# Three edits in a hybrid encoder kernel: the softmax division as a ScalarE copy, zero-padded low parts of the RWKV gate matrices, and the attention value projection over 512 columns in four banks

## The chip, the cores and the metric

The kernel runs on one NeuronCore of a Trainium2 chip. The metric is the device time of one execution in microseconds (us), as a median over runs. TensorE (PE in the profile; its weight loads are listed as PEld) multiplies matrices into PSUM, which has eight banks of 128 partitions by 512 float32 numbers. VectorE (DVE) and ScalarE (ACT) work element by element between PSUM and SBUF, GpSimd (POOL) sets constants and issues some of the transfers, and SyncE (SP) issues most of the others. Each engine works through its own list of instructions in order, and waits for others by semaphores.

## The reference, cut to what matters

Two layers over 1024 rows of width 1024. Layer 0 has a combined projection that feeds eight RWKV heads and eight heads of chunked band attention, and an output projection; layer 1 has a convolution module. Each layer ends with a squared-ReLU MLP of width 4096. The edits touch the attention's softmax and values and the decay and gate of RWKV.

```python
proj = h @ w_in
p_rwkv, q, k, v = jnp.split(proj, [RWKV_COLS, RWKV_COLS + ATT_WIDTH, RWKV_COLS + 2 * ATT_WIDTH], axis=-1)
...
w = -jax.nn.softplus(-(w0 + jnp.tanh(xw) @ w2)) - 0.5      # xw, xa: 64 columns each
decay = jnp.exp(-jnp.exp(w.astype(jnp.float32)))
a = jax.nn.sigmoid(a0 + xa @ a2)
...
s = jnp.where(valid[:, None, :], s, -1e30)
probs = jax.nn.softmax(s, axis=-1).astype(v.dtype)
o = jnp.einsum('bhcqk,bckhd->bcqhd', probs, vb)
...
x = x + sq_relu_mlp(rmsnorm(x, g_ffn), up, down)
```

## The kernel before

**Matmuls.** Nearly all matrix products are "dense" ones on split operands: each operand is a high part in a rounded 32-bit format (`xh`, `wh`) and a low part that holds the rest (`xl`, `wl`), and each product is the sum of three matmuls (L270 to L272): high by high, low by high, high by low. A weight part of 128 x 512 numbers arrives by a transfer that SP issues (`wr`), ScalarE rounds it to `wh` (L214), VectorE takes the difference `wl` (L215). Four `wh` and four `wl` buffers stand ready in the first 900 us.

**Halves.** The 1024 rows are worked in two halves of 512. For each half `w_in_gemm` projects the normalized rows: 22 tiles of 128 columns with the weights stationary (`gemm`), and then the attention's values, with the rows stationary and the weights moving, so that the values come out with rows on the partitions (L355 to L379). For the second half, `reload_x` fetches the rows back from DRAM (`xo`, four buffers) and splits them into eight pairs `xh[k]`, `xl[k]` (L163, L164), which take over the eight buffers of the first half's pairs.

**The value projection.** It takes 256 columns at a time. For each, four weight parts (two k steps each) are split, and then four row tiles run over all eight k steps, 24 matmuls of 256 columns each (L369 to L371). Two row tiles share a bank `d`. ScalarE copies each result out with the row's scale (L375) into `t1`, which has two buffers, and POOL writes it to `vd` in DRAM (L378).

**RWKV.** `rwkv` works 16 units in each of which two heads and 256 rows go through three stages (`prep`, `stage2`, `stage3`); the three stages of successive units are emitted interleaved. In `prep` the decay and the gate come from two small products each: `lora[0]` and `lora[1]` hold the rounded matrices w2 and a2, both copied into all 128 partitions, and meet the input's high part in one half of the partitions and its low part in the other (L488). `lora[2]` holds the low parts of both, w2's in partitions 0 to 63 and a2's in 64 to 127, and each product reads its own 64 (L491). `xdt` (the block inverses) and `wx` (the decays) exist twice, for units of even and odd number.

**Attention.** For every pair of heads and every 128 queries: scores of both heads (L808, L810) into a bank `a`, bias and row maximum on VectorE (L812), exponential with row sum on ScalarE (L819), reciprocal of the sum on VectorE (L820), transposes on TensorE (L830) copied out by ScalarE (L831), and products with the values, one head in each half of the columns (L837). The division comes last: a matmul of the reciprocals, broadcast along the columns, with the identity puts them beside the result (L840), ScalarE copies them to SBUF (L843) and VectorE multiplies (L844). Tag `a` has two banks.

**What sets the order.** A list scheduler places every instruction of every engine at build time by four levels: support (weights, evacuations), then the RWKV mixer, then attention, then dense matmuls, which fill what the others leave. `rwkv(0)` and `attention(0)` are emitted ahead of `w_in_gemm(1)`, and `rwkv(1)` and `attention(1)` ahead of the first half's output projection and MLP. Buffers of one tag pass from user to user in the order of the program.

Of the kernel before, what the change touches and what calls it, by code (L numbers as in the profile page):

```python
# [8 lines left out]
F32 = mybir.dt.float32  # L9
# [5 lines left out]
P = 128  # L15
D = 1024
SEQ = 1024
T = 512
# [43 lines left out]
def encoder_trunk(ctx: ExitStack, tc: tile.TileContext, x, vecs, consts, ext, w2a2, g2, w_in, w_out,  # L62
# [17 lines left out]
    def psum(tag):  # L80
        return ps[tag].tile([P, T], F32, tag=tag, name=tag)
# [67 lines left out]
    def boost():  # L149
        return At("support")  # L150

    def tmp(tag="t1"):
        return dpool.tile([P, T], F32, tag=tag, name=tag)
# [181 lines left out]
    def w_in_gemm(h, rhs, st, first=()):  # L335
        def evac(m, q, cols):
            rstd = st.rstd()
            s = tmp("t1")
            if Q0 <= m < K0:
                nc.vector.scalar_tensor_tensor(out=s[:], in0=q[:], scalar=0.125, in1=rstd[:],  # L340
                                               op0=ALU.mult, op1=ALU.mult)
            else:
                nc.vector.tensor_tensor(out=s[:], in0=q[:], in1=rstd[:], op=ALU.mult)
            ts = slice(h * T, (h + 1) * T)
            if Q0 <= m < V0:
                hi = tmp("t2")
                nc.scalar.copy(hi[:].bitcast(F32R), s[:])
                nc.vector.tensor_tensor(out=s[:].bitcast(F32R), in0=s[:], in1=hi[:], op=ALU.subtract)
                nc.gpsimd.dma_start(ph[m][:, ts], hi[:])
                nc.gpsimd.dma_start(pl[m][:, ts], s[:])  # L350
            else:
                nc.gpsimd.dma_start(pd[m][:, ts], s[:])

        gemm(w_in, 0, IN_ORDER, rhs, evac, st, first)
        for n0 in range(V0 * P, V0 * P + RW, 2 * P):  # L355
            parts = []
            with boost():
                for k0 in range(0, KT, 2):
                    parts.append(weight_part(w_in[k0 * P : (k0 + 2) * P, n0 : n0 + 2 * P], 2 * P))
            for t in range(4):  # L360
                if t % 2 == 0:
                    q = psum("d")
                cs = slice(t % 2 * 2 * P, (t % 2 + 1) * 2 * P)
                ts = slice(t * P, (t + 1) * P)
                with At("dense"):
                    for k in range(KT):
                        xh, xl = rhs[k]
                        hi, lo = (a[:].rearrange("p a b -> p (a b)")[:, k % 2 * 2 * P : (k % 2 + 1) * 2 * P] for a in parts[k // 2])
                        nc.tensor.matmul(q[:, cs], xh[:, ts], hi, start=(k == 0), stop=False)  # L369
                        nc.tensor.matmul(q[:, cs], xl[:, ts], hi, start=False, stop=False)  # L370
                        nc.tensor.matmul(q[:, cs], xh[:, ts], lo, start=False, stop=(k == KT - 1))  # L371
                with boost():
                    if t % 2 == 0:
                        s = tmp("t1")
                    nc.scalar.activation(s[:, cs], q[:, cs], AF.Copy, scale=st.part[1][:, t : t + 1])  # L375
                    if t % 2:
                        r0 = h * T + (t - 1) * P
                        nc.gpsimd.dma_start(vd[r0 : r0 + 2 * P, n0 - V0 * P : n0 - V0 * P + 2 * P].rearrange("(a p) c -> p a c", p=P),  # L378
                                            s[:].rearrange("p (a c) -> p a c", a=2))  # L379


    def rwkv(h, rp, nbuf):
        keep = {}
        for i in range(2):
            for n, w in (("xdt", C), ("wx", C + 1)):
                t = rp.tile([P, whole(NCH * w)], F32, tag=f"{n}{i}", name=f"{n}{i}")
                t = keep[n, i] = t[:, 0 : NCH * w].rearrange("p (c t) -> p c t", t=w)
                nc.gpsimd.memset(t, 0.0)
            t = keep["zs", i] = rp.tile([P, 2, C], F32, tag=f"zs{i}", name=f"zs{i}")
            nc.gpsimd.memset(t[:], 0.0)  # L390
# [19 lines left out]
    def rwkv_block(tb, rp, nbuf, keep):  # L410
# [60 lines left out]
        def prep(hp, u):  # L471
# [3 lines left out]
            wx = keep["wx", hp % 2]  # L475
# [13 lines left out]
            for i, q in enumerate((wps, aps)):  # L489
                s = slice(C * i, C * i + C)  # L490
                nc.tensor.matmul(q, lora[2][s, cs], lora_in[i][s, :], start=False, stop=True)  # L491
# [85 lines left out]
        def invert(u):  # L577
# [27 lines left out]
            xd16 = keep["xdt", hp % 2]  # L605
# [143 lines left out]
    def attention(h, ap):  # L749
# [3 lines left out]
        for hp in range(4):  # L753
# [27 lines left out]
            for qi in range(4):  # L781
# [18 lines left out]
                rr = []  # L800
                for hd in range(2):
# [19 lines left out]
                    rr.append(st[:, 4:5])  # L821
# [17 lines left out]
                for hd in range(2):  # L839
                    nc.tensor.matmul(ob[hd * C : hd * C + C, P : 2 * P], rr[hd].to_broadcast([P, C]), ident,  # L840
                                     start=True, stop=True)
                yo = ap.tile([P, P], F32, tag="yo", name="yo", bufs=1)
                nc.scalar.copy(yo[:], ob[:, P : 2 * P])  # L843
                nc.vector.tensor_tensor(out=yo[:], in0=ob[:, 0:P], in1=yo[:], op=ALU.mult)  # L844
# [200 lines left out]
    with banks(d=2, w=2, v=1, c=1, a=2), tc.tile_pool(name="lop", bufs=1) as lop, tc.tile_pool(name="wp1", bufs=4) as wb[0]:  # L1045
        lora = [lop.tile([P, RW], F32R, tag=f"lora{i}", name=f"lora{i}") for i in range(3)]
# [4 lines left out]
        with tc.tile_pool(name="xrp", bufs=4, reuse_waits="tile") as xrp:  # L1051
            with boost():
                xa, ra, sa, first = load_x(0, xrp)
                for i, s in enumerate((slice(0, C), slice(C, P))):
# [4 lines left out]
                    nc.vector.tensor_tensor(out=lora[2][s, :], in0=raw[s, :], in1=lora[i][s, :].bitcast(F32), op=ALU.subtract)  # L1059
# [130 lines left out]
```

## Time and profile before

| what | us |
|---|---|
| median of 3 runs (lowest, highest) | 2507.76 (2507.46, 2511.98) |
| the profiled execution | 2509.98 |
| its span in the profile | 2508.0 |
| PE, DVE, ACT, POOL busy | 2472.3, 1711.5, 1169.2, 118.4 |

In the rows of the profile a group is given as line, engine, operation, output and inputs by tile name, shapes and count; then busy time in us, mean duration of one in ns, and the idle time of the engine just before them with the instruction that ended most of it. For matmuls `128*64` is the stationary operand's rows and columns. A timeline row begins with its start and its duration in us. A float32 matmul that isn't on rounded operands shows as two passes. RWKV, attention and both projections lie in the first 900 us; what follows is MLPs and convolution.

### The profile page before, as it was taken

How to read it: one execution, taken by the hardware profiler on the slowest of the kernel's cores; microseconds unless marked ns; L12 is line 12 of the kernel's file. 1: busy time of each engine (PE TensorE's matmuls, PEld its weight loads, DVE VectorE, ACT ScalarE, POOL GpSimd, SP SyncE). 2: the span in 40 equal slices, each digit the busy share in tenths (PEclk: the TensorE clock that was granted, in tenths of full speed). 3: DMA queues.
4: the chain of work that ended last, by engine and by line, in shares of the span. 5: the costliest groups of instructions: out<-in, count | busy, mean ns of one | idle time of the engine just before them, and what ended most of it. 6: DMA issues, size and time to landing. Idle time of an engine off the chain costs nothing.

```text
span 2508.0 us, 38693 instructions
## 1 busy us (share of the span) xinstructions
PE 2472.3 (99%) x13532; PEld 1983.0 (79%) x13532; DVE 1711.5 (68%) x3559; ACT 1169.2 (47%) x2282; POOL 118.4 (5%) x285
## 2 busy tenths in 40 slices
PE   8999999999999999999999999999999999999998
PEld 6777677787777788888888888888888888888887
DVE  5687775677777644458999956599999475534434
ACT  5456565566775633343442334434432365423324
POOL 1111011100000000001100000000000000000000
PEclk9999999999999999999999999999999999999999
DMA  8543434543233233355333333533333334333332
GB/s 271 161 139 105 128 102 121 184 148 102 82 94 89 72 100 97 97 151 152 98 96 98 96 100 93 161 93 101 93 101 93 101 100 152 93 94 99 97 97 67
DMA packets 478514, 283.46 MB, mean 113 GB/s; under 512 B 44512, under 2 KB 457568, under 8 KB 478320
## 3 DMA queue, kind: packets, MB, share of 16 engines
q1 hardware_dynamic: 468128, 250.25, 34.1%
q0 software_dynamic: 9152, 29.36, 3.3%
q8 instruction: 107, 1.75, 0.3%
q10 hardware_dynamic: 1040, 1.38, 0.2%
q14 instruction: 87, 0.71, 0.1%
HBM read 247.31 MB, written 36.72 MB: 113 GB/s over the span
## 4 chain that ended last, share of the span: by engine, by line
PE 92%; DMA 3%; DVE 2%; ACT 2%; issue 1%; SPq 1%; ACTq 0%; DVEq 0%
PE d L272 26%; PE d L270 25%; PE d L271 25%; PE a L837 1%; PE w L556 1%; PE a L830 1%; PE v L633 1%; PE a L808 1%; DMA pt<-pd 1%; PE c L677 1%; PE c L689 1%; PE c L682 1%; PE a L810 1%; PE d L370 1%; PE d L369 1%
## 5 line engine op out<-in xcount | busy, mean ns | idle before, releaser
L214 ACT CAST wh<-wr 128x512 fp32r<-128x512 f32 x744 | 460.5, 621 | 971.5 <-PE d L271 898.8
L270 PE MATMUL d<-xh,wh 128*128 128x512 f32 x1872 | 743.6, 397 | 3.5 <-ACT xh L163 2.9
L272 PE MATMUL d<-xh,wl 128*128 128x512 f32 x1872 | 741.4, 396 | 1.2 <-DVE wl L215 1.2
L271 PE MATMUL d<-xl,wh 128*128 128x512 f32 x1872 | 739.7, 395 | 0.2 <-DVE xl L164 0.2
L215 DVE TENSOR_TENSOR wl<-wr,wh 128x512 fp32r<-128x512 f32 x744 | 501.6, 685 | 224.8 <-ACT wh L214 169.6
L270 PEld LDWEIGHTS d<-xh,wh 128*128 128x128 f32 x1872 | 353.5, 189 | 76.8 <-ACT xh L163 3.3
L272 PEld LDWEIGHTS d<-xh,wl 128*128 128x128 f32 x1872 | 353.1, 189 | 76.7 <-DVE wl L215 2.5
L271 PEld LDWEIGHTS d<-xl,wh 128*128 128x128 f32 x1872 | 353.5, 189 | 73.0 <-issue 1.2
L270 PE MATMUL d<-mh,wh 128*128 128x512 f32 (+1 forms) x1040 | 404.0, 388 | 0.0
L272 PE MATMUL d<-mh,wl 128*128 128x512 f32 (+1 forms) x1040 | 402.6, 387 | 0.0
L271 PE MATMUL d<-ml,wh 128*128 128x512 f32 (+1 forms) x1040 | 402.3, 387 | 0.0
L964 DVE SCALAR_TENSOR_TENSOR cv<-u,dwt,cv 128x512 f32<-128x512 f32 x480 | 331.9, 743 | 0.7
L272 PEld LDWEIGHTS d<-mh,wl 128*128 128x128 f32 x1040 | 195.3, 188 | 38.8
L270 PEld LDWEIGHTS d<-mh,wh 128*128 128x128 f32 x1040 | 195.3, 188 | 38.7
L271 PEld LDWEIGHTS d<-ml,wh 128*128 128x128 f32 x1040 | 195.4, 188 | 38.6
L863 DVE TENSOR_TENSOR x<-d,x 128x512 f32<-128x512 f32 (+1 forms) x146 | 97.6, 679 | 155.5 <-PE d L272 155.2
L905 DVE SCALAR_TENSOR_TENSOR t<-d,rstd 128x512 f32<-128x512 f32 x128 | 86.4, 687 | 119.6 <-PE d L272 116.8
L911 DVE TENSOR_TENSOR ml<-t,mh 128x512 fp32r<-128x512 f32 x128 | 87.7, 687 | 20.0 <-ACT mh L909 17.3
L907 ACT ACTIVATE t<-t 128x512 f32<-128x512 f32 x128 | 80.1, 626 | 17.9 <-DVE t L905 17.6
L909 ACT ACTIVATE mh<-t 128x512 fp32r<-128x512 f32 x128 | 78.9, 616 | 0.0
L181 DVE TENSOR_TENSOR acc<-acc,t 128x512 f32<-128x512 f32 (+1 forms) x86 | 57.9, 673 | 9.4 <-ACT t L180 9.1
L687 ACT ACTIVATE sd<-vs,dc 64x64 f32<-64x64 f32 x128 | 44.2, 346 | 33.5 <-DVE vs L692 25.8
(265 smaller groups left out, 2439.8 us busy)
## 6 DMA issues: line engine op xcount, KB each, us to landing
wr<-in_up_dram SPq DMA_DIRECT2D x256, 256.0 KB
wr<-in_dn_dram SPq DMA_DIRECT2D x256, 256.0 KB
wr<-in_w_in_dram SPq DMA_DIRECT2D x104, 256.0 KB
wr<-in_pw_dram SPq DMA_DIRECT2D x96, 256.0 KB
wr<-in_w_out_dram SPq DMA_DIRECT2D x32, 256.0 KB
pd<-t POOLq DMA_DIRECT2D x28, 256.0 KB, 2.7
x<-xd SPq DMA_DIRECT2D x24, 256.0 KB
pt<-pd SPq DMA_DIRECT2D x42, 128.5 KB
```

Of the source, the lines that this page charges most:

```text
L181: nc.vector.tensor_tensor(out=self.acc[:, cols], in0=self.acc[:, cols], in1=sq[:, cols], op=ALU.add)
L214: nc.scalar.copy(hi[:], raw[:])
L215: nc.vector.tensor_tensor(out=lo[:], in0=raw[:], in1=hi[:].bitcast(F32), op=ALU.subtract)
L270: nc.tensor.matmul(q[:, cols], hi, xh[:, cols], start=(k == 0), stop=False)
L271: nc.tensor.matmul(q[:, cols], hi, xl[:, cols], start=False, stop=False)
L272: nc.tensor.matmul(q[:, cols], lo, xh[:, cols], start=False, stop=(k == KT - 1))
L863: nc.vector.tensor_tensor(out=xs[m][:, cols], in0=q[:, cols], in1=xs[m][:, cols], op=ALU.add)
L905: nc.vector.scalar_tensor_tensor(out=t[:], in0=q[:], scalar=0.0, in1=rstd[:], op0=ALU.max, op1=ALU.mult)
L907: nc.scalar.activation(sq[:], t[:], AF.Square)
L909: nc.scalar.activation(hi[:], t[:], AF.Square)
L911: nc.vector.tensor_tensor(out=lo[:], in0=sq[:], in1=hi[:].bitcast(F32), op=ALU.subtract)
L964: nc.vector.scalar_tensor_tensor(out=c[:], in0=u[:, tap : tap + T], scalar=dw(tap), in1=c[:], op0=ALU.mult, op1=ALU.add)
```

## The change

Softmax: ScalarE multiplies the exponentials by the reciprocal in place, in SBUF, ahead of the transposes. The 64 matmuls with the identity and ScalarE's copies of their results go, and VectorE's last multiplication becomes a copy out of PSUM.

Gates: the low parts get a tile of their own each, `lora[2]` and `lora[3]`, with zeros in the 64 partitions that hold the input's low part, and the second matmul reads all 128 partitions. To make room, `xdt` and `wx` exist once.

Values: k is the outer loop. Each weight part is 128 rows by all 512 columns, and four accumulators of 512 columns, one per row tile, stay open over all of k, in the two banks `d` and the two banks `a`. Four results of 128 x 512 are copied out at the end.

```diff
         gemm(w_in, 0, IN_ORDER, rhs, evac, st, first)
-        for n0 in range(V0 * P, V0 * P + RW, 2 * P):
-            parts = []
-            with boost():
-                for k0 in range(0, KT, 2):
-                    parts.append(weight_part(w_in[k0 * P : (k0 + 2) * P, n0 : n0 + 2 * P], 2 * P))
-            for t in range(4):
-                if t % 2 == 0:
-                    q = psum("d")
-                cs = slice(t % 2 * 2 * P, (t % 2 + 1) * 2 * P)
-                ts = slice(t * P, (t + 1) * P)
-                with At("dense"):
-                    for k in range(KT):
...
-                    if t % 2 == 0:
-                        s = tmp("t1")
-                    nc.scalar.activation(s[:, cs], q[:, cs], AF.Copy, scale=st.part[1][:, t : t + 1])
...
+        qs = [psum(tag) for tag in SPARE]
+        for k in range(KT):
+            with boost():
+                hi, lo = (a[:].rearrange("p a b -> p (a b)")
+                          for a in weight_part(w_in[k * P : (k + 1) * P, V0 * P : V0 * P + RW], RW))
+            xh, xl = rhs[k]
+            with At("dense"):
+                for t, q in enumerate(qs):
+                    ts = slice(t * P, (t + 1) * P)
+                    nc.tensor.matmul(q[:], xh[:, ts], hi, start=(k == 0), stop=False)
+                    nc.tensor.matmul(q[:], xl[:, ts], hi, start=False, stop=False)
+                    nc.tensor.matmul(q[:], xh[:, ts], lo, start=False, stop=(k == KT - 1))
+        with boost():
+            for t, q in enumerate(qs):
+                s = tmp("t1")
+                nc.scalar.activation(s[:], q[:], AF.Copy, scale=st.part[1][:, t : t + 1])
+                nc.gpsimd.dma_start(vd[h * T + t * P : h * T + (t + 1) * P, :], s[:])
...
-            for i, q in enumerate((wps, aps)):
-                s = slice(C * i, C * i + C)
-                nc.tensor.matmul(q, lora[2][s, cs], lora_in[i][s, :], start=False, stop=True)
+                nc.tensor.matmul(q, lora[2 + i][:, cs], lora_in[i][:], start=False, stop=True)
...
-                    rr.append(st[:, 4:5])
+                    nc.scalar.activation(pt[:, 0:w], pt[:, 0:w], AF.Copy, scale=st[:, 4:5])
...
-                for hd in range(2):
-                    nc.tensor.matmul(ob[hd * C : hd * C + C, P : 2 * P], rr[hd].to_broadcast([P, C]), ident,
-                                     start=True, stop=True)
-                nc.scalar.copy(yo[:], ob[:, P : 2 * P])
-                nc.vector.tensor_tensor(out=yo[:], in0=ob[:, 0:P], in1=yo[:], op=ALU.mult)
+                nc.vector.tensor_copy(yo[:], ob[:, 0:P])
...
-        lora = [lop.tile([P, RW], F32R, tag=f"lora{i}", name=f"lora{i}") for i in range(3)]
+        lora = [lop.tile([P, RW], F32R, tag=f"lora{i}", name=f"lora{i}") for i in range(4)]
+        for i in range(2):
+            nc.gpsimd.memset(lora[2 + i][C - C * i : P - C * i, :].bitcast(F32), 0.0)
...
-                    nc.vector.tensor_tensor(out=lora[2][s, :], in0=raw[s, :], in1=lora[i][s, :].bitcast(F32), op=ALU.subtract)
+                    nc.vector.tensor_tensor(out=lora[2 + i][s, :], in0=raw[s, :], in1=lora[i][s, :].bitcast(F32), op=ALU.subtract)
```

The scheduler's order moves with it. Three places follow. Line numbers of the change are its own: there the value matmuls are L364 to L366, their copies L370, the gate matmuls L480 and L481, scores L797 and L799, exponential L808, the division's copy L810, transposes L819, value products L826.

ACT at the end of the first half's value projection, before: L163 makes the second half's `xh`, L375 copies the last value result, L214 rounds weights, the rest belongs to RWKV and attention.

```order
L680 COPY zs_1658<-c 64x64
L657 COPY vs<-v 128x2x192
L163 ACTIVATE xh<-xo,vec 128x512 x4
L214 CAST wh<-wr 128x512
L375 ACTIVATE t_1480<-d,rc 128x256
L214 CAST wh<-wr 128x512 x2
L163 ACTIVATE xh<-xo,vec 128x512 x2
L214 CAST wh<-wr 128x512
L163 ACTIVATE xh<-xo,vec 128x512 x2
L214 CAST wh<-wr 128x512
```

The same place in the change: the last two of the eight L163 and the four result copies L370, from banks `d` and `a`.

```order
L163 ACTIVATE xh<-xo,vec 128x512
L603 COPY vs<-v 128x2x64
L370 ACTIVATE t_1399<-d,rc 128x512
L370 ACTIVATE t_1402<-d,rc 128x512
L677 ACTIVATE sd<-vs,dc 64x64 x2
L670 COPY zs_1555<-c 64x64
L214 CAST wh<-wr 128x512
L163 ACTIVATE xh<-xo,vec 128x512
L674 COPY vs<-c 64x64
L421 ACTIVATE e<-pt,vec 128x256
L370 ACTIVATE t_1405<-a,rc 128x512
L370 ACTIVATE t_1408<-a,rc 128x512
```

Before, eight splits stand together at the end; now six of them stand further up, among the projection's own weights, and the third and fourth result copies stand behind RWKV's small copies.

PE where the second half's value projection ends, before (the next rows are the first half's output projection):

```order
L369 MATMUL d<-wh,xh 128x256
L370 MATMUL d<-wh,xl 128x256
L371 MATMUL d<-wl,xh 128x256
L270 MATMUL d<-xh,wh 128x512
L271 MATMUL d<-xl,wh 128x512
L272 MATMUL d<-xh,wl 128x512
```

The same place in the change, with L446 of RWKV and the first scores of the second half's attention:

```order
L366 MATMUL a<-wl,xh 128x512
L270 MATMUL d<-xh,wh 128x512
L271 MATMUL d<-xl,wh 128x512
L272 MATMUL d<-xh,wl 128x512
L270 MATMUL d<-xh,wh 128x512
L271 MATMUL d<-xl,wh 128x512
L272 MATMUL d<-xh,wl 128x512
L446 MATMUL w<-cst,e 128x128 x2
L270 MATMUL d<-xh,wh 128x512
L271 MATMUL d<-xl,wh 128x512
L272 MATMUL d<-xh,wl 128x512
L797 MATMUL a<-kk,qq 128x320
```

Before, scores of the second half stand ahead of and inside its value projection; now the first of them follows nine dense matmuls behind it. The first half's last value product stands 60 matmuls of 128x512 ahead of the second half's value projection.

ACT in the second half's attention, before: two exponentials (L819), and the copies of the transposed tiles (L831).

```order
L819 ACTIVATE pt,st<-pt,st 128x640
L684 COPY vs<-c 64x64
L819 ACTIVATE pt,st<-pt,st 128x640
L214 CAST wh<-wr 128x512
L687 ACTIVATE sd<-vs,dc 64x64 x2
L680 COPY zs_6272<-c 64x64
L831 COPY pT<-a 128x512
L831 COPY pT<-a 128x128
```

Such a place in the change, with the division's copies (L810):

```order
L808 ACTIVATE pt,st<-pt,st 128x640
L214 CAST wh<-wr 128x512
L670 COPY zs_6057<-c 64x64
L677 ACTIVATE sd<-vs,dc 64x64 x2
L214 CAST wh<-wr 128x512
L674 COPY vs<-c 64x64
L810 ACTIVATE pt<-pt,st 128x640
L639 COPY bkt<-v 128x512
L808 ACTIVATE pt,st<-pt,st 128x640
L810 ACTIVATE pt<-pt,st 128x640
```

The copy stands after other work behind the first exponential and directly behind the second. On PE, between a head's last score matmul and its first transpose, there stand 22 matmuls of 128x512 in the mean before and 27 now.

More of the change, by code (lines that the diff above doesn't have):

```diff
@@ L354, in w_in_gemm @@
         gemm(w_in, 0, IN_ORDER, rhs, evac, st, first)
-        for n0 in range(V0 * P, V0 * P + RW, 2 * P):
-            parts = []
+        qs = [psum(tag) for tag in SPARE]
+        for k in range(KT):
             with boost():
-                for k0 in range(0, KT, 2):
-                    parts.append(weight_part(w_in[k0 * P : (k0 + 2) * P, n0 : n0 + 2 * P], 2 * P))
-            for t in range(4):
-                if t % 2 == 0:
-                    q = psum("d")
-                cs = slice(t % 2 * 2 * P, (t % 2 + 1) * 2 * P)
-                ts = slice(t * P, (t + 1) * P)
-                with At("dense"):
-                    for k in range(KT):
[L367 to L371, printed above, removed]
-                with boost():
-                    if t % 2 == 0:
-                        s = tmp("t1")
[L375 to L379, printed above, removed]
@@ L382, in rwkv @@
+        with boost():
[3 more added lines that the diff above has]
+                nc.gpsimd.dma_start(vd[h * T + t * P : h * T + (t + 1) * P, :], s[:])
     def rwkv(h, rp, nbuf):
         keep = {}
+        for n, w in (("xdt", C), ("wx", C + 1)):
+            t = rp.tile([P, whole(NCH * w)], F32, tag=n, name=n)
+            t = keep[n] = t[:, 0 : NCH * w].rearrange("p (c t) -> p c t", t=w)
+            nc.gpsimd.memset(t, 0.0)
@@ L384, in rwkv @@
         for i in range(2):
[L385 to L388, printed above, removed]
             t = keep["zs", i] = rp.tile([P, 2, C], F32, tag=f"zs{i}", name=f"zs{i}")
@@ L474, in prep @@
                 yield
-            wx = keep["wx", hp % 2]
+            wx = keep["wx"]
             cs = slice(P * hp, P * hp + P)
@@ L604, in invert @@
                                   xi[C * hd : C * hd + C, :, :].rearrange("p a b -> p (a b)"))
-            xd16 = keep["xdt", hp % 2]
+            xd16 = keep["xdt"]
             for hd in range(2):
@@ L799, in attention @@
                 pr = []
-                rr = []
                 for hd in range(2):
```

## The prediction, made before the result was known

> **What bounds the kernel now.** I read the page first (busy shares and the chain that ended last), then the busy time by stretch, then single stretches of TensorE's timeline. From the page:
>
> ```profile
> span 2508.0 us, 38693 instructions
> PE 2472.3 (99%) x13532; PEld 1983.0 (79%) x13532; DVE 1711.5 (68%) x3559; ACT 1169.2 (47%) x2282; POOL 118.4 (5%) x285
> PE 92%; DMA 3%; DVE 2%; ACT 2%; issue 1%; SPq 1%; ACTq 0%; DVEq 0%
> ```
>
> TensorE is busy for 99% of the span and holds 92% of the last chain, so a matmul taken from it shortens the run unless a new wait takes its place. Five stretches of the span (columns: stretch, its length, busy time of PE, PEld, DVE, ACT and POOL with instruction counts, clock, DMA share, GB/s):
>
> ```profile
> 0.00:30.00 30.00, 22.03 (x92) 15.59 (x93) 17.00 (x30) 16.99 (x33) 1.19 (x12) 1.00 0.83 269
> 30.00:100.00 70.00, 63.99 (x300) 50.39 (x298) 37.73 (x73) 34.87 (x64) 13.15 (x43) 0.95 0.71 227
> 100.00:900.00 800.00, 786.88 (x5974) 591.53 (x5975) 572.24 (x1731) 496.68 (x1127) 73.65 (x198) 0.99 0.39 114
> 900.00:2400.00 1500.00, 1499.07 (x6667) 1240.72 (x6667) 1039.33 (x1642) 579.53 (x979) 30.43 (x32) 1.00 0.36 106
> 2400.00:2508.00 108.00, 100.29 (x505) 84.73 (x503) 45.22 (x85) 41.13 (x82) 0.00 (x0) 0.98 0.26 80
> ```
>
> All three edits work in the first 900 us. There TensorE is idle for 8 + 6 + 13 = 27 us, and 13 of them lie in 100 to 900. From 900 to 2400 it runs 6667 matmuls in 1500 us, 0.225 us from start to start: the price of one 128x512 matmul. Durations in the rows are longer (0.39 us) because neighbours overlap, so every price below is a difference of start times.
>
> **The division's matmuls (L840).** They go: 64 in the code, 128 passes.
>
> ```profile
> L840 PE MATMUL a<-cst,st 128*64 128x128 f32 x128 | 21.4, 277 | 0.0
> 411.94 0.27 PE L840 MATMUL a<-cst,st 128*64 128x128 f32 x1
> 411.95 0.27 PE L837 MATMUL a<-pT,vt 128*64 128x128 f32 x1
> 412.05 0.27 PE L840 MATMUL a<-cst,st 128*64 128x128 f32 x1
> 412.06 0.27 PE L837 MATMUL a<-pT,vt 128*64 128x128 f32 x1
> 412.17 0.38 PE L840 MATMUL a<-cst,st 128*64 128x128 f32 x2
> 412.48 0.50 PE L808 MATMUL a<-kk,qq 128*128 128x512 f32 x1
> 250.14 0.38 PE L840 MATMUL a<-cst,st 128*64 128x128 f32 x2
> 250.46 0.33 PE L653 MATMUL v<-cst,vp 128*128 128x128 f32 x1
> 251.46 0.43 PE L840 MATMUL a<-cst,st 128*64 128x128 f32 x2
> 251.82 0.44 PE L808 MATMUL a<-kk,qq 128*128 128x384 f32 x1
> ```
>
> At 411.94 the first head's two passes start within 0.01 us of the other head's value matmuls (L837): they cost nothing. Only the second head's two stand alone, from 412.17 on; with steps of 0.11 us they are worth 0.23 us. Over 32 groups that is 7 us. At 250.14 the four stand apart from everything: 0.32 + 0.36 = 0.68 us, which over 32 groups would be 22 us, about the 21.4 us of the grouped row. Most groups that I looked at are like the first, so I take 10 us, with ends 7 and 21.
>
> **The gate's low parts (L491).** Same number of matmuls, but over 128 rows instead of 64.
>
> ```profile
> 200.72 0.50 PE L272 MATMUL d<-xh,wl 128*128 128x512 f32 x1
> 201.06 0.28 PE L488 MATMUL w<-xl,lora 128*128 128x256 f32 x1
> 201.27 0.38 PE L491 MATMUL w<-xl,lora 64*128 64x256 f32 x1
> 201.58 0.50 PE L270 MATMUL d<-xh,wh 128*128 128x512 f32 x1
> 205.69 0.28 PE L369 MATMUL d<-wh,xh 128*128 128x256 f32 x1
> 205.81 0.28 PE L370 MATMUL d<-wh,xl 128*128 128x256 f32 x1
> 205.93 0.28 PE L371 MATMUL d<-wl,xh 128*128 128x256 f32 x1
> ```
>
> A 256-column matmul between matmuls of its own shape takes 0.12 us (205.69 to 205.81). The pair L488, L491 takes 0.21 + 0.31 = 0.52 us: 0.1 us is lost when the stationary shape changes to 64 rows and about 0.2 us on L491 and the way back. With one shape the pair should take 0.24 us, and 32 pairs give 32 x 0.28 = 9 us. The ends are 9 and 5, for pairs that stand beside another small shape anyway. The Trainium skill (TensorE: Matmul & The Clock Gate, section "Why this matters for your kernels") speaks against this edit: it has matmuls with few rows put into separate row groups, where they run at the same time. By that rule 16 pairs of low parts would share 0.12 us each and padding would give 2 us back, a sum 2 us worse; the trace does not agree, since after L491 the next matmul starts 0.31 us later and none runs beside it.
>
> **The value projection.** 384 matmuls of 256 columns become 192 of 512: 384 x 0.12 = 46 us against 192 x 0.225 = 43 us, so 3 us less; I take 2, with ends 3 and 0. Bytes and number of weight and result transfers stay. The larger effect is one of order. Now every weight column block passes over all the normalized rows, so the last use of each `xh[k]` comes at the very end, and the next half's `xh` are made in one burst (the ACT rows in the part on the change). Three rows, of ACT, of PE and of the stretches:
>
> ```profile
> 263.35 1.51 ACT L163 ACTIVATE xh<-xo,vec 128x512 fp32r<-128x512 f32 x2 [3.49 <-DMA xo<-xd]
> 264.12 0.58 PE L270 MATMUL d<-xh,wh 128*128 128x512 f32 x1 [2.85 <-ACT xh L163]
> 264.00:272.00 8.00, 7.67 (x23) 4.76 (x23) 5.26 (x12) 3.91 (x11) 0.58 (x1) 0.57 0.42 123
> ```
>
> ACT waits 3.49 us for reloaded rows whose buffers came free late, TensorE 2.85 us for ACT, and then the granted clock is 0.57 for 8 us: another 0.43 x 8 = 3.4 us. With k outermost, `xh[k]` is free after its 12 matmuls, an eighth of the way at a time, and the new ACT order spreads the eight splits over the projection. I take the whole 6 us as gone; ends 6 and 0.
>
> Against it stands a new wait. Four results leave through `t1`, which has two buffers, so the third evacuation waits until the first has landed in DRAM:
>
> ```profile
> vd<-t POOLq DMA_DIRECT2D x8, 256.0 KB, 3.4
> L378 POOL DMA_DIRECT2D vd<-t x8 | 5.7, 717 | 38.0 <-ACT t L375 31.6 <-ACT e L452 3.6 <-ACT yo L843 2.8
> ```
>
> An evacuation of some 0.6 us and 3.4 us to landing make 4.0 us; the third bank is full 6 x 0.225 = 1.4 us after the first, so ACT stands 2.7 us. Queued behind it on ACT are the RWKV chain's small copies and the next softmax, and on TensorE the first scores, which need those banks; ahead of the scores stand nine dense matmuls (2 us). Twice about 1 us: +2, with ends 0 and 6.
>
> **The division on ScalarE.**
>
> ```profile
> L819 ACT ACTIVATE pt<-pt,st 128x640 f32<-128x640 f32 (+4 forms) x64 | 44.5, 695 | 9.5 <-DVE st L818 8.6
> L1003 ACT ACTIVATE t<-x,vec 128x512 f32<-128x512 f32 (+1 forms) x18 | 11.9, 660 | 0.0
> L843 ACT COPY yo<-a 128x128 f32<-128x128 f32 x32 | 8.5, 265 | 27.1 <-PE a L840 27.0
> L820 DVE RECIPROCAL st<-st 128x1 f32<-128x1 f32 x64 | 9.9, 155 | 12.4 <-ACT pt L819 11.9
> L830 PE MATMUL a<-cst,pt 128*128 128x128 f32 x240 | 42.1, 281 | 1.1 <-ACT pt L819 0.9
> ```
>
> 64 scaled copies at 0.66 us (L1003 is the same operation at a like size) are 42 us on ACT, against 8.5 us of L843 that go; ACT has 800 - 497 = 303 us free between 100 and 900. The path of a head grows by reciprocal and copy, 0.155 + 0.66 = 0.82 us. I cost it at nothing: dense matmuls stand between scores and transposes, 27 in the mean where 22 stood, five more or 1.1 us. Without that cover it is 64 x 0.82 = 52 us. DVE's last step changes one 128x128 operation for another. The single `xdt` and `wx` cost nothing as long as units stay apart: 16 units in 800 us are 50 us each, and what would wait is small transfers on SP, ahead of weights that are fetched early.
>
> The sum: -10 - 9 - 2 - 6 + 2 = -25 us. The profiled execution took 2509.98 us, with a span of 2508.0; the median of the runs is 2507.76, so the span serves as the median: 2483 us.
>
> **The rivals.** (a) *Only the matmul work counts:* the burst of reloads finds another place to wait, and L840 is worth its lower end. -7 - 9 - 2 + 2 = -16: 2492. For it: each half's reload still goes over DRAM, beside 114 GB/s of other traffic. (b) *The groups of four mostly stand alone:* -21 - 9 - 2 - 6 + 2 = -36: 2472. (c) *Four banks tie the projection to the attention,* so nothing is gained:
>
> ```profile
> L808 PE MATMUL a<-kk,qq x96: 218/386/504, 177.4 to 861.2; 128*128 128x320 f32 x32, 128*128 128x128 f32 x16, 128*128 128x256 f32 x16, 128*128 128x384 f32 x16
> L843 ACT COPY yo<-a x7: 265/267/267, 400.4 to 452.5; 128x128 f32<-128x128 f32 x7
> 504.88 0.28 PE L369 MATMUL d<-wh,xh 128*128 128x256 f32 x1
> 256.24 0.47 ACT L375 ACTIVATE t<-d,rc 128x256 f32<-128x256 f32 x1
> ```
>
> The first half's attention runs from 177.4 to 452.5, 275 us, partly beside its own projection; the second projection starts at 504.9. Two of the banks are the attention's own, so it can now start only when the projection has ended (in the trace its last evacuation starts at 256.24), and the second projection only when it has ended. If it kept its 275 us it would end at 532, 27 us late, and the 25 us would be gone: 2508 to 2510. Against it: 60 dense matmuls, 13.5 us, stand between its last value matmul and the second projection. (d) *The softmax wait lands on TensorE,* the slower side: behind an exponential in ACT's order stand weight casts, and the 52 us come in full: 2483 + 52 = 2535. It decides once TensorE stands more than 25 us ahead of the transposes, 0.39 us per head; it stands 1.1 us now. The Trainium skill (ScalarE: Activation LUTs, section "Rules for kernel authors") sides with it: multiplications belong on VectorE. Here the stretch from 100 to 900 has DVE busy for 572 us and ACT for 497, so the trace does not bear it out.
>
> **How the numbers follow.** Forecast 53%, (a) 20%, (b) 10%, (c) 10%, (d) 7%. Three of them, 83%, are faster by well over 0.2% (5 us, about what a measurement of this kernel can tell from no change), and (c) lies near zero and leaves a little to both sides: faster 0.84, same 0.09, slower 0.07. The range takes in forecast, (a), (b) and the better edge of (c): 2471 to 2502; of (c) and (d) some 16% is left out.
>
> **What would show it.** Right: PE busy near 2450; L840 gone, the second gate matmul about 0.12 us behind the first; no 2.85 us wait on `xh` and no stretch with a clock of 0.57 after the first projection; ACT waits for the landing of the first result ahead of the third evacuation, but transposes (now L819) idle for a few us in all. Wrong: idle time of tens of us ahead of the transposes, or TensorE idle ahead of the second projection with its releaser among the attention's copies.

## The result and the profile after

The changed kernel takes 2485.61 us (median of 4 runs, 2484.63 to 2486.04), the kernel before beside it 2509.2 us: a ratio of 0.9904 with a 95% interval of 0.9887 to 0.9922, so 20 to 28 us faster. The profiled execution took 2485.57 us, with a span of 2483.8. The page of the changed kernel (span, busy times, chain that ended last):

```profile
span 2483.8 us, 38039 instructions
PE 2447.5 (99%) x13212; PEld 1955.1 (79%) x13212; DVE 1707.5 (69%) x3559; ACT 1196.5 (48%) x2306; POOL 115.8 (5%) x283
PE 92%; DMA 3%; DVE 2%; ACT 1%; issue 1%; SPq 0%; ACTq 0%; DVEq 0%
```

TensorE is still the bound, with 320 matmul passes fewer (128 of the division, 192 of the values). Its busy time fell by 24.8 us and the span by 24.2: the idle time of TensorE did not change. The same stretches as before (stretch, length, busy times with counts, clock, DMA share, GB/s):

```profile
0.00:30.00 30.00, 21.11 (x86) 15.02 (x87) 15.90 (x28) 15.28 (x30) 2.23 (x14) 0.96 0.85 268
30.00:100.00 70.00, 61.30 (x292) 48.86 (x292) 37.70 (x70) 34.81 (x64) 12.44 (x40) 0.92 0.73 223
100.00:900.00 800.00, 790.02 (x5776) 585.35 (x5774) 580.01 (x1750) 533.01 (x1167) 68.76 (x188) 1.00 0.40 117
900.00:2400.00 1500.00, 1499.07 (x6667) 1241.20 (x6666) 1037.24 (x1640) 578.52 (x975) 32.40 (x42) 1.00 0.36 106
```

From 100 to 900 TensorE is idle for 10 us instead of 13, at full clock. From 30 to 100 it is idle for 8.7 us instead of 6.0, and the clock is lower, 0.92 instead of 0.95. The waits of TensorE (total, times, longest) and three groups of instructions of the changed kernel say where:

```profile
PE w L480 <- DVE xl L461: 7.4, 2, 6.9
PE w L446 <- ACT e L444: 4.2, 3, 2.4
PE d L364 <- DVE t L343: 1.6, 1, 1.6
```

```profile
L480 PE MATMUL w<-xl,lora 128*128 128x256 f32 x32 | 10.8, 340 | 7.4 <-DVE xl L461 7.4
L481 PE MATMUL w<-xl,lora 128*128 128x256 f32 x32 | 9.3, 293 | 0.0
L163 ACT ACTIVATE xh<-xo,vec 128x512 fp32r<-128x512 f32 x8 | 5.8, 720 | 0.0
```

The largest wait is now at the first gate matmul of the program (L480); its counterpart in the kernel before, from the same view:

```profile
PE w L488 <- DVE xl L469: 5.3, 2, 4.4
```

L446 spreads head sums over rows, L364 is the first matmul of a value group. No wait on `xh` is left: the eight splits of the second half's rows (L163) stand idle for 0.0 us, where ACT had waited 3.49 us for reloaded rows before. TensorE's timeline of the changed kernel (start, duration, line, shape, idle time before it), a clean gate pair first, then the first gate matmul:

```profile
206.27 0.28 PE L480 MATMUL w<-xl,lora 128*128 128x256 f32 x1
206.38 0.28 PE L481 MATMUL w<-xl,lora 128*128 128x256 f32 x1
206.50 0.40 PE L365 MATMUL d<-wh,xl 128*128 128x512 f32 x1
...
69.43 0.39 PE L270 MATMUL d<-xh,wh 128*128 128x512 f32 x1
76.76 0.55 PE L480 MATMUL w<-xl,lora 128*128 128x256 f32 x1 [6.94 <-DVE xl L461]
77.11 0.42 PE L481 MATMUL w<-xl,lora 128*128 128x256 f32 x1
77.32 0.63 PE L271 MATMUL d<-xl,wh 128*128 128x512 f32 x1
77.75 0.63 PE L272 MATMUL d<-xh,wl 128*128 128x512 f32 x1
78.18 0.63 PE L270 MATMUL d<-xh,wh 128*128 128x512 f32 x1
```

A pair takes 0.23 us beside its own shape. Behind the wait of 6.94 us the dense matmuls stand 0.43 us apart instead of 0.227: half clock, which the trace's clock record gives for 10.2 us from 72.0 on (before: 6.8 us from 73.3 on). It begins within the wait, which lasts from 69.8 to 76.8, so 4.8 of the 10.2 us pass while TensorE has nothing to do.

### The profile page after: what moved, and what is told of

It is laid out like the page before. It is cut to its first block, busy times and chain, and to the rows that moved or that the text cites. A ratio compares the mean times of both kernels' runs of the same rounds, so it can differ in the third digit from the quotient of the medians.

```text
span 2483.8 us, 38039 instructions
## 1 busy us (share of the span) xinstructions
PE 2447.5 (99%) x13212; PEld 1955.1 (79%) x13212; DVE 1707.5 (69%) x3559; ACT 1196.5 (48%) x2306; POOL 115.8 (5%) x283
## 4 chain that ended last, share of the span: by engine, by line
PE 92%; DMA 3%; DVE 2%; ACT 1%; issue 1%; SPq 0%; ACTq 0%; DVEq 0%
PE d L272 26%; PE d L270 26%; PE d L271 26%; PE a L826 1%; PE w L546 1%; PE a L819 1%; PE v L623 1%; PE a L797 1%; PE c L667 1%; DMA pt<-pd 1%; PE c L679 1%; PE c L672 1%; PE a L799 1%; DVE wl L215 1%; DMA nb<-msc 0%
## 5 line engine op out<-in xcount | busy, mean ns | idle before, releaser
L214 ACT CAST wh<-wr 128x512 fp32r<-128x512 f32 x744 | 461.1, 621 | 954.3 <-PE d L271 866.7
L677 ACT ACTIVATE sd<-vs,dc 64x64 f32<-64x64 f32 x128 | 44.2, 346 | 31.7 <-DVE vs L682 21.3
```

The lines of the kernel that those rows point to most:

```text
L214: nc.scalar.copy(hi[:], raw[:])
```

## The experiments

One method serves all runs. From the page come the span and TensorE's busy time; from the trace's clock record the stretches at a clock of 0.5. Half of the time for which TensorE is busy in such a stretch is lost; its idle time there already stands in the idle column. What is left of the busy time is called matmul work here: busy time minus this loss. All times in us; the intervals are for the ratio to the kernel before, run on the same chip. Span and the last three columns are of one profiled execution, which lies up to 3 us from the median (e2 and e5). The expectations of e10, e11 and e12 give matmul work by a coarser count that takes idle time at half clock off as well: their 7.1, 3.5, 13.4 and 8.0 us are 8.4, 3.3, 13.1 and 5.2 in this table.

| kernel | median | ratio (95%) | span | PE idle | lost to half clock | matmul work |
|---|---|---|---|---|---|---|
| before | 2507.8 | | 2508.0 | 35.8 | 7.9 | 2464.4 |
| the change | 2485.6 | 0.9904 (0.9887 to 0.9922) | 2483.8 | 36.3 | 4.4 | 2443.1 |
| e1 softmax | 2497.7 | 0.9955 (0.9941 to 0.9968) | 2493.9 | 34.4 | 3.4 | 2456.0 |
| e2 gates | 2500.6 | 0.9967 (0.9955 to 0.9980) | 2501.8 | 43.8 | 6.7 | 2451.3 |
| e3 values | 2496.3 | 0.9951 (0.9939 to 0.9964) | 2494.0 | 29.4 | 3.4 | 2461.1 |
| e4 values, 256 columns | 2501.2 | 0.9966 (0.9954 to 0.9979) | 2499.2 | 31.0 | 3.4 | 2464.8 |
| e5 division twice | 2484.9 | 0.9902 (0.9888 to 0.9915) | 2486.1 | 34.2 | 6.3 | 2445.5 |
| e6 division on VectorE | 2491.2 | 0.9927 (0.9913 to 0.9940) | 2489.4 | 35.8 | 7.3 | 2446.3 |
| e7 results over two tags | 2492.1 | 0.9927 (0.9915 to 0.9940) | 2490.2 | 35.5 | 6.0 | 2448.8 |
| e8 bias rows later | 2492.4 | 0.9929 (0.9917 to 0.9942) | 2491.0 | 36.5 | 6.2 | 2448.3 |
| e9 one pair of bias rows | 2493.4 | 0.9941 (0.9928 to 0.9954) | 2491.4 | 35.2 | 8.0 | 2448.2 |
| e10 softmax and values | 2492.3 | 0.9940 (0.9927 to 0.9954) | 2489.3 | 31.1 | 1.7 | 2456.4 |
| e11 gates and values | 2494.9 | 0.9949 (0.9935 to 0.9964) | 2492.0 | 34.5 | 9.8 | 2447.7 |
| e12 before, bias rows later | 2512.0 | 1.0008 (0.9999 to 1.0017) | 2511.0 | 37.5 | 8.2 | 2465.3 |

How well the last column repeats can be seen from e8 and e9: TensorE, ScalarE and VectorE run the same instructions in the same order there, and their matmul work differs by 0.1 us.

The theory was that of the prediction: the parts have a price each, and these add. The first rival was that only matmul work counts and waits come back elsewhere.

### The parts alone

**e1, softmax alone**, the rest as before:

```diff
+ nc.scalar.activation(pt[:, 0:w], pt[:, 0:w], AF.Copy, scale=st[:, 4:5])
- nc.tensor.matmul(ob[hd * C : hd * C + C, P : 2 * P], rr[hd].to_broadcast([P, C]), ident, ...)
- nc.scalar.copy(yo[:], ob[:, P : 2 * P])
- nc.vector.tensor_tensor(out=yo[:], in0=ob[:, 0:P], in1=yo[:], op=ALU.mult)
+ nc.vector.tensor_copy(yo[:], ob[:, 0:P])
```

> The kernel before with the softmax edit alone (division as a ScalarE copy ahead of the transposes, no matmuls with the identity). Theory of the prediction: -10 us against before (ends -7 and -21), all of it matmul time, and TensorE idle for no more than a few us ahead of the transposes. Rival (waits fell differently, the edits do not add up): within 4 us of before alone. Rival (softmax wait on TensorE): slower by 20 us or more.

Measured: 11.1 us faster. The time fits the forecast of 10, but only 8.4 us of it is matmul work (2464.4 to 2456.0); 4.5 us came from half clock and 1.4 from idle time, which add up to more than the 11.1 of the medians because they are of single executions. The wait on the reloaded rows, which this run was to leave alone, shrinks as well:

```profile
PE d L270 <- ACT xh L163: 0.5, 1, 0.5
```

**e2, gates alone:**

```diff
- nc.tensor.matmul(q, lora[2][s, cs], lora_in[i][s, :], start=False, stop=True)
+ nc.tensor.matmul(q, lora[2 + i][:, cs], lora_in[i][:], start=False, stop=True)
- keep["wx", hp % 2], keep["xdt", hp % 2]
+ keep["wx"], keep["xdt"]
```

> The kernel before with the gate edit alone (zero-padded low parts over 128 rows, single xdt and wx). Theory: -9 us (ends -5 and -9), since each second gate matmul starts 0.12 us behind the first and the next one 0.12 us later. Rival (64-row matmuls in separate row groups ran at the same time, so padding loses that): +2 us. Rival (single xdt and wx hold the units up): between 0 and -4 us.

Measured: 8.3 us faster, with 13.1 us less matmul work and 8.0 us more idle time on TensorE, in an execution 3 us above the median. The longest wait is the first gate matmul's, 6.6 us; what TensorE waits for the products of the single `xdt` is 0.8 us, where it was 0.6. No wait on `xh` is left here either.

**e3, values alone:**

```diff
- for n0 in range(V0 * P, ...): for t in range(4): for k in range(KT): ...   # 256 columns
+ qs = [psum(tag) for tag in SPARE]
+ for k in range(KT): for t, q in enumerate(qs): ...                          # 512 columns
```

> The kernel before with the value projection edit alone (512 columns, k outermost, four banks). Theory: -2 for the columns, -6 for the reload wait that goes, +2 for the new evacuation wait: -6 us; no wait of TensorE on xh behind the first projection. Rival (four banks tie projection and attention): 0 to +20 us, with idle time ahead of the second projection. Rival (the wait goes elsewhere): -2 us.

Measured: 12.6 us faster, twice the 6 expected; 3.3 us of it is matmul work, and some 6 us of idle time and 4.5 us of half clock go as well. No wait on `xh` is left.

**e4, the new loops of e3 with 384 matmuls of 256 columns:**

```diff
- nc.tensor.matmul(q[:], xh[:, ts], hi, start=(k == 0), stop=False)
+ for cs in (slice(0, 2 * P), slice(2 * P, 4 * P)):
+     nc.tensor.matmul(q[:, cs], xh[:, ts], hi[:, cs], start=(k == 0 and cs.start == 0), stop=False)
```

> The kernel before with the value projection in the new loop order and the four banks, but still in matmuls of 256 columns (384 of them). Theory: it keeps the order's share and loses the columns' share, so 2 to 3 us above the edit alone at 512 columns, and 3 to 4 us below before. Rival (the gain is in the wide matmuls, not in the order): equal to before.

Measured: 7.7 us faster, with the matmul work of before (2464.8 against 2464.4). So the gain of the new loop order comes from idle time and half clock alone, and the wide matmuls are worth 3.7 us beside it (2464.8 to 2461.1). The two halves of the value edit have the signs that the prediction gave them, and both are larger: 7.7 us against 3 to 4, and 4.9 in the medians against 2 to 3. Whether the first of them belongs to the loop order is not shown, since e1, e2 and e12 lose the same wait without it (0.5, 0 and 0.9 us are left of the 2.9).

The three parts alone give 11.1 + 8.3 + 12.6 = 32 us, the whole change 24. The matmul work nearly adds: 8.4 + 13.1 + 3.3 = 24.8 against 21.3. What does not add at all is idle time and half clock: the singles save 6 and 11 us of them (e1, e3) and lose 7 (e2), the whole change saves 3.

### The pairs

**e10, softmax and values; e11, gates and values:** two of the three edits above, the third left as before.

```diff
  e10 = e1 + e3
  e11 = e2 + e3
```

> The kernel before with the softmax division and the value projection changed, the gates as before. Alone these two gave -11.1 and -12.6 us, of which -7.1 and -3.5 us is matmul work; the rest is idle time and half clock, much of it at the first gate matmul (wait 2.8 and 2.6 us there, 4.4 before). If both had shrunk the same wait by a new order, it is counted twice: -10.6 of work and once some -8 to -10 of waits: 2488 to 2490 us. If they add: 2485. If the gain of the waits is only a matter of each order and is lost in another: 2496 to 2499.

> The kernel before with the gates and the value projection changed, the softmax division as before. Matmul work -13.4 - 3.5 = -17 us. If the value projection's waits (-10.4 us alone) are its own: -27 us, 2482 us. If they are given back as in the whole change: -17 us, 2492 us. If the single results add (-8.3 - 12.6): 2488 us.

Measured: 15 us faster (e10) and 13 us (e11) by the ratios, where the singles add up to 23.7 and 20.9. In e10 the saved waits stay: idle time 4.7 and half clock 6.2 us lower than before, but the matmul work is 3.7 us above what its parts add up to. In e11 the matmul work is as added (2447.7 against 2448.0), and the waits are back: 1.3 us less idle, 1.9 us more half clock. So e10 falls in none of the three cases exactly (between the first and the third), and e11 a little beyond the second. With the pairs, the matmul work of each part can be read beside different others. The gates take 13.1 us alone, 13.4 beside the values (e3 to e11) and 13.3 beside both (e10 to the change): that is their own. The division takes 8.4 us alone, but 4.7 and 4.6 beside the values (e3 to e10, e11 to the change): these two are not worth their sum. The waits belong to no part.

### Does the division land on TensorE?

**e5, every head divided twice:**

```diff
  nc.scalar.activation(pt[:, 0:w], pt[:, 0:w], AF.Copy, scale=st[:, 4:5])
+ nc.scalar.activation(pt[:, 0:w], pt[:, 0:w], AF.Copy, scale=ones[:, 0:1])
```

> The changed kernel with the ScalarE copy of every head done twice (the second one multiplies by a column of ones): 64 more copies of 0.77 us, 49 us more on ScalarE, each in the path from the scores to the transposes. My theory, that five more dense matmuls per head (1.1 us) cover the division: the second copy needs 0.77 us more than that cover holds (0.16 + 0.77 + 0.77 = 1.7 us), but the order of the matmuls is made anew with the longer copy in it, so more dense matmuls come to stand there; 0 to +5 us against the changed kernel's 2485.6. Rival (d) of the prediction, that the time comes in full on TensorE: +49 us, 2535.

Groups of instructions of e5 (L811 is the second copy, L820 the transposes):

```profile
L811 ACT ACTIVATE pt<-pt,ones 128x640 f32<-128x640 f32 (+4 forms) x64 | 44.3, 694 | 0.8
L810 ACT ACTIVATE pt<-pt,st 128x640 f32<-128x640 f32 (+4 forms) x64 | 44.1, 692 | 3.5 <-DVE st L809 2.8 <-DVE st L807 0.2
L820 PE MATMUL a<-cst,pt 128*128 128x128 f32 x240 | 41.4, 280 | 0.3 <-ACT pt L811 0.3
```

44.3 us more on ScalarE, and TensorE waits 0.3 us ahead of the transposes; the time is that of the changed kernel (2484.9). The order was made anew around the longer copy and found more dense matmuls to stand there: 27 in the mean between the last score matmul of a pair of heads and its first transpose, where the changed kernel has 20. Rival (d) falls, with room to spare for a second copy.

**e6, the division on VectorE:**

```diff
- nc.scalar.activation(pt[:, 0:w], pt[:, 0:w], AF.Copy, scale=st[:, 4:5])
+ nc.vector.tensor_scalar(pt[:, 0:w], pt[:, 0:w], st[:, 4:5], None, op0=ALU.mult)
```

> The changed kernel with the division as one VectorE tensor_scalar instead of the ScalarE copy, nothing else changed: 64 operations move from ScalarE (48% busy) to VectorE (69% busy). My theory, that the division lies under dense matmuls and TensorE is the bound: within 3 us of the changed kernel's 2485.6. By the Trainium skill (ScalarE: Activation LUTs, section Rules for kernel authors) multiplications belong on VectorE: a few us faster, if ScalarE's order is what delays the transposes. Rival, that VectorE is the fuller engine in 100 to 900 us: 5 to 10 us slower.

Two groups of e6, the division and the transposes behind it:

```profile
L810 DVE TENSOR_SCALAR pt<-pt,st 128x640 f32<-128x640 f32 (+4 forms) x64 | 29.8, 466 | 1.2
L819 PE MATMUL a<-cst,pt 128*128 128x128 f32 x240 | 41.1, 283 | 0.1
```

One division takes 0.466 us there instead of 0.69, and the transposes wait 0.1 us. Still the time is 5.6 us above the changed kernel, as the rival of a fuller VectorE asked for, but not for its reason: idle time is 0.5 us lower, half clock takes 2.9 more, and 3.2 us is matmul work. That pointed to the order itself.

### The new waits

**e7, third and fourth result through the other tag:**

```diff
- s = tmp("t1")
+ s = tmp("t1" if t < 2 else "t2")
```

> The changed kernel with the third and fourth result of each value projection written through the buffers of the other tag, so that the third evacuation does not wait for the first result's landing. In the changed kernel this wait is 1.1 us on ScalarE and 0.9 us on TensorE ahead of the first scores in all. My theory: 0 to -2 us. Rival, that the wait also makes the order around it worse: -5 us.

The copies of the value results (L370) of the changed kernel, and what waits before and behind them (us, times):

```profile
L370 ACT ACTIVATE t<-d,rc x4: 687/690/695, 232.8 to 511.9; 128x512 f32<-128x512 f32 x4
...
  DMA vd<-t: 1.1, 2
...
  PEld a L797: 0.9, 2
```

In e7 the wait of 1.1 us is gone, and the 0.9 us ahead of the scores is 0.3. So the wait costs about 1 us, where the prediction had 2. The whole time is 6.5 us higher all the same, where 0 to 2 less were expected, with 5.7 us more matmul work: the wait that was taken away cannot cost that.

**e8, bias rows later.** The changed kernel waits 6.9 us at the first gate matmul. Ahead of it POOL writes eight broadcast bias rows, and VectorE stands for the landing of projected rows (POOL and VectorE in the timeline of the changed kernel):

```profile
53.16 4.15 POOL L1059 DMA_DIRECT2D ext<-rows  x8 [4.16 <-DMA rows<-es]
60.18 0.56 POOL L352 DMA_DIRECT2D pd<-t  x1 [2.87 <-DMA ext<-rows]
70.89 0.69 DVE L343 TENSOR_TENSOR t<-d,rstd 128x512 f32<-128x512 f32 x1 [5.86 <-DMA pd<-t]
```

```diff
- for i in range(8): ... nc.gpsimd.dma_start(t[:, 0:EXTW], ...)
+ extend(0)                                       # heads 0 and 1
  # in attention, per head pair:
+ if h == 0 and hp < 3: extend(2 * hp + 2)
```

> The changed kernel with six of the eight broadcast writes of the attention's bias rows (L1059, 0.38 MB each) issued one head pair ahead of their use instead of all together at 53 us. In the changed kernel they and the weight loads lie ahead of the rows (pt<-pd) that the first gate matmul needs; TensorE waits 6.9 us for it at 69.8 us, and its clock is then half for 10.2 us. If that traffic is the cause of the wait: -5 to -10 us (2476 to 2481), and no wait over 4 us ahead of L480. If the wait comes from the order of the queue alone or from VectorE's work on the second half's rows: 0 to -2 us, wait unchanged.

It did only a part of what it was to do: all eight writes were still issued by 70 us, and TensorE still waits 6.3 us at L480, though it comes to it earlier, at 68.9 us instead of 76.8. It left the question open, and showed one thing more: 6.7 us slower than the changed kernel, 5.2 us of it matmul work, with not one matmul more.

**e9, one pair of DRAM buffers,** so that a write has to follow the bias loads of the head pair before:

```diff
- extd.append(dram.tile(...))                     # eight, written at once
+ pair = [dram.tile(...) for i in range(2)]       # written again for every head pair
- e0 = extd[hh][:]
+ e0 = extend(hh)[:]
```

> The changed kernel with one pair of DRAM buffers for the broadcast bias rows instead of four pairs: each pair of writes (2 x 0.38 MB) now has to follow the bias loads of the head pair before, so that 1.5 MB are written around 53 to 75 us instead of 3.1 MB, and the rest during the attention (both halves write them, 6.1 MB in all). In the run with later writes all eight still went out by 70 us, so it did not take the traffic away; this one does. If that traffic is what makes the first gate matmul wait (6.9 us, and 10.2 us at half clock): the wait falls below 3 us and the time to 2475 to 2480 us. If the wait has another cause: wait unchanged, 2485 to 2493 us, where the three last edits with hardly a cost of their own came out.

Waits of TensorE in e9, then the row of its timeline that ends the second of them, and the same row of e8:

```profile
PE a L797 <- DMA kk<-pl: 4.3, 3, 2.8
PE w L480 <- DVE xl L461: 4.0, 2, 3.2
```

```profile
64.95 0.36 PE L480 MATMUL w<-xl,lora 128*128 128x256 f32 x1 [3.16 <-DVE xl L461]
```

```profile
68.87 0.55 PE L480 MATMUL w<-xl,lora 128*128 128x256 f32 x1 [6.31 <-ACT wh L214]
```

The wait falls to 3.2 us, a little above the 3 us that were set. The run to compare with is e8, which has the same order on TensorE, ScalarE and VectorE: 6.3 to 3.2 us, so in that order, and with one execution of each, the traffic makes up about half of the wait. The start of this matmul says the same: 74 to 78 us in the eleven kernels that issue all eight writes at once, 68 and 69 in e12 and e8, 65 in e9. But how long TensorE waits there is set by the order as much as by the traffic: among those eleven it is 0.5 us (e10), 2.6 (e3) and up to 6.9. The time does not follow: two new stretches at half clock, 6.8 us each at 424 and 479 us, take the gain back. Into the first of them falls a wait of 2.8 us for attention rows (`kk`), 3 us after two of the moved writes were issued; e8 has no wait there. As a way to a faster kernel it failed.

### What an order is worth

**e12, the edit of e8 on the kernel before:** the same lines as e8, in the unchanged kernel.

```diff
- for i in range(8): ... nc.gpsimd.dma_start(t[:, 0:EXTW], ...)
+ extend(0)
+ if h == 0 and hp < 3: extend(2 * hp + 2)
```

> The kernel before with the same edit as the run with later writes (six of the eight broadcast writes issued with the head pair before), nothing else. On the changed kernel it added 6 to 7 us, 8.0 us of it matmul work, although no matmul is added: only the order of the instructions was made anew. If an order alone is worth several us in either direction, this kernel differs from the kernel before by 3 to 10 us, faster or slower, with the same 13532 matmuls and another matmul work than its 2460.4 us. If the edit itself costs 6 to 7 us, it is slower by as much here: 2515 us. If orders are equal: within 2 us.

Measured: 1.0008 (0.9999 to 1.0017), so 2 us slower, 4 at most, which can't be told from none, with nearly the same matmul work (0.9 us more). The pages of e12 and e8 (span and busy times):

```profile
span 2511.0 us, 38725 instructions
PE 2473.5 (99%) x13532; PEld 1986.2 (79%) x13532; DVE 1710.3 (68%) x3559; ACT 1169.0 (47%) x2282; POOL 113.8 (5%) x285
```

```profile
span 2491.0 us, 38038 instructions
PE 2454.5 (99%) x13212; PEld 1957.4 (79%) x13212; DVE 1710.1 (69%) x3559; ACT 1201.3 (48%) x2308; POOL 115.7 (5%) x283
```

So the edit itself does not cost the 6.7 us that e8 lost, and the guess that every new order moves the time by 3 us or more does not hold for the kernel before. What is shown: the changed kernel and e5 to e9 run the same 13212 matmuls in five orders (e8 and e9 share one), and their matmul work goes from 2443.1 to 2448.8 us, the changed kernel's being the lowest. The mean of their six ratios is 0.9922, some 20 us below the kernel before. With the reserve that e5 to e9 have small costs of their own, I read 20 us as what the three edits bring, and the last 4 as the order that they happened to get. Why one order has less matmul work than another is open in the main. Counted from start to start, the value products take 40 us in the changed kernel, e5 and e6 and 42 to 43 in e7 to e9; the rest is spread over many lines. The three with the most changes of the stationary shape from one matmul to the next (693 in e7, 694 in e8 and e9, against 683 in the changed kernel) have the most, but e6 has the fewest, 680, and 3.2 us more than the changed kernel.

No run beats the changed kernel by more than the measurement can tell (e5 is 0.7 us below it).

## Why the prediction was right, and where its steps were not

The time of 2483 us was 2.6 too low, and the range of 2471 to 2502 held it. The sum came out by terms that missed in both directions:

| term | predicted | measured |
|---|---|---|
| division's matmuls | -10 (-21 to -7) | -8.4 (matmul work of e1) |
| gate pairs | -9 (-9 to -5) | -13.1 (matmul work of e2) |
| 512 columns | -2 (-3 to 0) | -3.3 (matmul work of e3) |
| reload wait, and new result wait | -6 + 2 | -3.0 (idle time and half clock of the whole change) |
| what the parts' matmul work adds to beyond the whole's | | +3.5 |
| sum | -25 | -24.3 (spans) |

- **Division's matmuls.** The choice that failed was to take 10 between the ends: e1 shows 8.4, nearer to the lower end of 7. And the sum took the parts as independent, where beside the values the division is worth only 4.6 (e11 to the change). Counted from start to start, L840 takes 16.5 us in the kernel before, but the value products take 7.6 us more in e1 than before, 40.8 instead of 33.2. So nearly half of L840's time goes over to them. Rival (b), 21 us, falls with it.
- **Gate pairs.** The price of the pair was right: the two gate matmuls take 17.5 us from start to start in the kernel before and 9.5 in e2, 0.25 us less for each pair against 0.28. What the prediction left out stands outside the pair. A dense matmul directly behind L491 takes 0.345 us, behind the padded one 0.253; 23 of the 32 pairs have one there, some 2 us in all. About 3 us more lie elsewhere and are not explained; as the 13.1 us come again beside other edits (13.4 and 13.3), they are hardly a chance of one order. The Trainium skill (TensorE: Matmul & The Clock Gate, section "Why this matters for your kernels"), which has matmuls with few rows put into separate row groups to run at the same time, would have made padding a loss; e2 is 8.3 us faster, so for these pairs the measurement decides against it.
- **512 columns.** A little beyond its best end of 3; e4 shows with its unchanged matmul work that it is the width that counts.
- **The reload wait** is gone as forecast: no idle time is left on L163, and neither is the half clock at 264. The reason given for it is not shown. In e1, e2 and e12 the old value projection still makes its splits in a burst (247 to 257 us in e1, 254 to 265 in e2), and TensorE waits 0.5, 0 and 0.9 us there: most of the 2.9 us belonged to one order and went with it. The step "I take the whole 6 us as gone" also left out that other waits come: the first gate matmul waits 6.9 us instead of 4.4, L446 waits 4.2 instead of 1.4 at its counterpart L447, and L364 1.6. In sum idle time rose by 0.5 us and half clock fell by 3.5, so -3.0 where the forecast had -4. Rival (a), "the burst of reloads finds another place to wait", is right in that waits came back, though it is no reload that waits; its 2492 was not reached, since the matmul work fell by 21.3 us where it had 18, and the waits by 3.0 where it had 2 more.
- **The new result wait** has the place that was foretold, ScalarE ahead of the third copy and TensorE ahead of the first scores, and costs about 1 us instead of 2.
- **The division on ScalarE** at nothing was right: the transposes wait 0.3 us in the changed kernel, and e5 shows cover for a second copy. The cover is not a fixed number of dense matmuls, as the prediction had counted it (27 for 22); the order is made with the copy's length in it.
- **Rival (c)** falls: the second value projection starts at 480.26 (first row below, changed kernel's timeline) where the kernel before started it at 504.88, and its one wait, on the projection's own copies, is 1.6 us.

```profile
480.26 0.39 PE L364 MATMUL d<-wh,xh 128*128 128x512 f32 x1
482.94 0.50 PE L364 MATMUL d<-wh,xh 128*128 128x512 f32 x1 [1.61 <-DVE t L343]
```

So the forecast was near partly by luck, because the errors cancel: +1.6 on the division, -4.1 on the gates, -1.3 on the columns, +1.0 on the waits, +3.5 of remainder.

## What to carry to other kernels

Where TensorE is busy for 99% of the span, an edit's price is the matmul time that it takes away, and it is priced best by start-to-start steps, those of its neighbours too; a wait that an edit removes should be booked as gained only if the next wait behind it is named. Where a scheduler makes the order, every edit draws a new one: here that was worth up to 6 us of matmul work among five orders of the same matmuls, and any one wait could come or go. A gain of that size is shown by its coming again beside other edits, as the gates' did, and not by one run. A copy that a scheduler sees coming can be nearly free: a second one of 44 us was.

## What the hardware showed that was not expected

Half clock comes in pieces of one length, on a fixed beat. The stretches in the clock record are 3.41, 6.83 and 10.24 us, one, two or three times 3.41 (only the last one of each run, at its end, has another length), and within a run they begin whole multiples of 3.41 us apart: at 73.3, 264.4 and 472.6 us in the kernel before, 56 and 61 pieces. So a stretch can begin within a wait, as in the changed kernel at 72.0, and what it costs is not set by the length of the wait. Behind the 6.9 us at the first gate matmul, about 5.5 of the 10.24 us fell on work, 2.7 us lost; the 3.2 us of e9 were followed by one piece, 1.7 us lost, and the 2.85 us in the kernel before by two, 3.3 us lost. The 2.4 us at L446 in the changed kernel were followed by none; the beat cuts them at 491.8, into 1.9 and 0.5 us. In all 14 traces, after the first 20 us, every piece of this beat, but the last of a run, in which TensorE was idle for 2.0 us or more was followed by one at half clock; of those with less idle time, some were and some not.

The Trainium skill (TensorE: Matmul & The Clock Gate, section "What's actually happening") has the clock set by a free-running window of 3413 ns, and the lengths and the beat agree; it has the clock fall after at least one idle window, some 3.4 us, where 2.0 us of idle time within a window were enough here; there the trace decides.
